# A sparse 3x3 convolution on one core: the seventh pair stored in halves, three input loads moved

## The chip, the core and the metric

The kernel runs on one core of a Trainium2 chip. The metric is the device time of one execution in microseconds (us); lower is better. The core has five engines with their own instruction streams: TensorE (PE in the profile, with its weight loads as PEld), VectorE (DVE), ScalarE (ACT), GpSimd (POOL) and SyncE (SP). DMA transfers are issued by SP and by POOL here and are moved by the core's 16 DMA engines.

## The reference

The input `x` is 16 images of 64 channels of 64 x 64 float32; `weight` is 128 x 64 x 3 x 3, nine tenths of it zero. With a padding of one pixel on each side:

```python
for b in range(batch):
    for co in range(c_out):
        for ci in range(c_in):
            for kh in range(k):
                for kw in range(k):
                    if weight[co, ci, kh, kw] != 0:
                        output[b, co] += weight[co, ci, kh, kw] * x_pad[b, ci, kh:kh+h, kw:kw+w]
```

The kernel computes it as a dense convolution. It reads 16.8 MB of float32 input and writes 33.6 MB of float32 output.

## The kernel before

**Tiling.** Two images make a pair: their 2 x 64 channels fill the 128 partitions. There are 8 pairs (numbered 0 to 7), and each pair is worked in 4 blocks of 16 output rows, so 32 blocks, `b` = 0 to 31. `xs` holds all 8 pairs in bf16 at once, so no load waits for a buffer. The output of a pair is built in one of three float32 tiles `os` (`p % 3`), 4 MB each.

**A block.** POOL adds neighbouring input rows into `s` (line 178), ACT copies the block's 18 rows into `win` (line 211), and PE makes three products from them (line 292): `ps_p`, shared by even and odd output rows, then `ps_e` and `ps_o`. ACT copies `ps_p` to `pc` (line 219); DVE adds it to `ps_e` and to `ps_o` and writes the even and odd rows of the output tile (line 248). A block takes PE 3.24 us.

**Stores.** After the last block of a pair DVE writes a small tile `mark` (line 254) whose only use is to raise the semaphore `r`. SP's stream is a list of stores, each waiting for its value of `r`: one store of 4 MB for each of pairs 0 to 6 (lines 116 to 119), and two of 2 MB, rows 0 to 31 and rows 32 to 63, for pair 7 (lines 121 to 128), the first of them after block 29. A whole store moves in runs of 16 KB, a half in runs of 8 KB. Before DVE writes the first block of pair 3 or later it waits until the store that last read the same output tile has landed (`st0` to `st2`, line 246).

**Loads.** SP loads the weights and the first 32 rows of pair 0 in float32. All other input comes through POOL's DMA queue, which converts float32 to bf16 on the way. POOL's stream holds these issues in a fixed order: the rest of pair 0, pairs 1 to 3 and 24 rows of pair 4 at the start, and the others behind the addition of a given block, by the table `AT` (lines 157 to 163): the rest of pair 4 behind block 6 (and after pair 0's output is complete), pair 5 behind block 10, pair 6 behind block 14, and the halves of pair 7 behind blocks 18 and 22. The semaphores of the loads are `x0` to `x4` (`p % 5`); POOL's addition and ACT's copy of a pair's first block wait for the value in `X_LANDS` (line 103). For pair 7 that is 48, so both its halves must have landed before block 28.

**End.** After the blocks, SP waits for all stores (lines 313 to 317).

Of the kernel before, what the change touches and what calls it, by code (L numbers as in the profile page):

```python
# [17 lines left out]
def kernel(  # L18
# [20 lines left out]
    TURN = 2  # L39
    HEAD = 32  # L40
    CUT = 24
    N_O = 3

    pool = ctx.enter_context(tc.tile_pool(name="all", bufs=1))
# [55 lines left out]
    def x_sem(p):  # L100
        return f"x{p % 5}"

    X_LANDS = {0: 16, 1: 16, 2: 16, 3: 16, 4: 32, 5: 32, 6: 32, 7: 48}
    HEAD_R, HEAD_C, HEAD_Q = 8, 4, 3
    R_OF = {p: HEAD_R + p + 1 for p in range(NP - 1)}

    with tc.tile_critical(no_gpsimd_drain=True):  # L107
        with nc.Block(no_gpsimd_drain=True) as block:  # L108

            @block.sync  # L110
            def _(sp):
                sp.dma_start(  # L112
                    out=w_sb, in_=weight.rearrange("o i kh kw -> o (i kh kw)")
                ).then_inc(S("w"), 16)
                sp.dma_start(out=x_head, in_=pair(0)[:, 0:HEAD, :]).then_inc(S("xh"), 16)
                for p in range(NP - 1):
                    after(
                        sp.dma_start(out=out_of(p), in_=os[p % N_O]), ("r", R_OF[p])
                    ).then_inc(S(f"st{p % N_O}"), 16)
                p = NP - 1  # L120
                for h in range(2):
                    rows = slice(32 * h, 32 * h + 32)
                    after(
                        sp.dma_start(
                            out=out_of(p)[:, :, rows, :], in_=os[p % N_O][:, :, rows, :]
                        ),
                        ("r", HEAD_R + NP + h),
                    ).then_inc(S("st7" if h else f"st{p % N_O}"), 16)

            @block.gpsimd  # L130
            def _(gp):
                def load(p, a, b, *waits):
                    after(
                        gp.dma_start(out=xs[:, p, a + 1 : b + 1, :], in_=pair(p)[:, a:b, :]), *waits  # L134
                    ).then_inc(S(x_sem(p)), 16)

                load(0, HEAD, H)
                gp.memset(ident, 0.0).then_inc(S("s"), 1)
                after(
                    gp.affine_select(  # L140
                        out=ident,
                        in_=ident,
                        compare_op=mybir.AluOpType.not_equal,
                        fill=1.0,
                        base=0,
                        pattern=[[-1, 128]],
                        channel_multiplier=1,
                    ),
                    ("s", 1),
                ).then_inc(S("s"), 1)  # L150
                for p in range(1, 4):
                    load(p, 0, H)
                load(4, 0, CUT)
                for _ in range(16):
                    gp.nop()

                AT = {
                    6: (4, CUT, H, ("r", R_OF[0])),
                    10: (5, 0, H),
                    14: (6, 0, H),  # L160
                    18: (7, 0, 32),
                    22: (7, 32, H),
                }
                for b in range(NB):
                    p, r0 = b // 4, 16 * (b % 4)
                    waits = []
                    if b == 0:
                        waits.append(("xh", 16))
                    if b == 2 or (b % 4 == 0 and b):
                        waits.append((x_sem(p), X_LANDS[p]))  # L170
                    if b >= 2:
                        waits.append(("p", b - 1))
                    if b < 2:
                        src = x_head[:, r0 : r0 + 16, :]
                    else:
                        src = xs[:, p, r0 + 1 : r0 + 17, :]
                    after(
                        gp.tensor_tensor(  # L178
                            out=ss[b % 2], in0=src[:, 0:16:2, :], in1=src[:, 1:16:2, :], op=ADD
                        ),  # L180
                        *waits,
                    ).then_inc(S("s"), 1)
                    if b in AT:
                        load(*AT[b])

            @block.scalar
            def _(act):
                after(cast_w(act.copy, G1, 3, 4), ("w", 16)).then_inc(S("c"), 1)
                cast_w(act.copy, G2, 0, 3).then_inc(S("c"), 1)
                after(act.copy(out=wT[:, G1], in_=wps(G1)), ("q", 1)).then_inc(S("c"), 1)  # L190
                after(act.copy(out=wT[:, G2], in_=wps(G2)), ("q", 3)).then_inc(S("c"), 1)

                def window(b):
                    p, r0 = b // 4, 16 * (b % 4)
                    parts = [(xs[:, p, r0 : r0 + 18, :], 0, [])]
                    if b == 0:
                        parts = [(x_head[:, 0:17, :], 1, [("xh", 16)])]
                    elif b == 1:
                        parts = [
                            (x_head[:, 15:32, :], 0, []),  # L200
                            (xs[:, 0, 33:34, :], 17, [(x_sem(0), X_LANDS[0])]),
                        ]
                    elif b == 2:
                        parts = [(x_head[:, 31:32, :], 0, []), (xs[:, 0, 33:50, :], 1, [])]
                    elif b % 4 == 0:
                        parts[0][2].append((x_sem(p), X_LANDS[p]))
                    if b >= 2:
                        parts[0][2].append(("q", HEAD_Q + 2 * (b - 2) + 2))
                    for k, (src, a, waits) in enumerate(parts):
                        copy = after(  # L210
                            act.copy(out=win[b % 2][:, a : a + src.shape[1], :], in_=src), *waits  # L211
                        )
                        if k == len(parts) - 1:
                            copy.then_inc(S("x"), 1)

                window(0)
                window(1)
                for b in range(NB):
                    after(act.copy(out=pcs[b % 2], in_=ps_p[b % 2]), ("p", b + 1)).then_inc(S("c"), 1)  # L219
                    if b + 2 < NB:  # L220
                        window(b + 2)

            @block.vector
            def _(dve):
                dve.memset(idle_rhs, 0.0).then_inc(S("r"), 1)  # L225
                dve.memset(xs[:, :, 0 : H + 2 : H + 1, :], 0.0)
                dve.memset(win[0][:, 0:1, :], 0.0).then_inc(S("r"), 1)
                after(cast_w(dve.tensor_copy, G1, 0, 3), ("w", 16)).then_inc(S("r"), 1)
                cast_w(dve.tensor_copy, G0, 0, 3)
                cast_w(dve.tensor_copy, G0, 3, 4).then_inc(S("r"), 1)  # L230
                cast_w(dve.tensor_copy, G2, 3, 4).then_inc(S("r"), 1)
                after(dve.tensor_copy(out=wT[:, G0], in_=wps(G0)), ("q", 2)).then_inc(S("r"), 1)  # L232
                after(
                    dve.tensor_tensor(out=wT[:, G01], in0=wps(G0), in1=wT[:, G1], op=SUB), ("c", 3)
                ).then_inc(S("r"), 1)
                after(
                    dve.tensor_tensor(out=wT[:, G21], in0=wps(G2), in1=wT[:, G1], op=SUB), ("c", 4)
                ).then_inc(S("r"), 1)
                for b in range(NB):
                    p, r0 = b // 4, 16 * (b % 4)  # L240
                    for k, src in enumerate((ps_e, ps_o)):
                        waits = [("q", HEAD_Q + 2 * b + k + 1)]
                        if k == 0:
                            waits.append(("c", HEAD_C + b + 1))
                            if b % 4 == 0 and p >= N_O:
                                waits.append((f"st{p % N_O}", 16 * (p // N_O)))
                        after(
                            dve.tensor_tensor(  # L248
                                out=os[p % N_O][:, :, r0 + k : r0 + 16 : 2, :], in0=src, in1=pcs[b % 2], op=ADD
                            ),  # L250
                            *waits,
                        ).then_inc(S("eo"[k]), 1)
                    if b % 4 == 3 or b == NB - 3:
                        dve.memset(mark, 0.0).then_inc(S("r"), 1)

            @block.tensor
# [54 lines left out]
                        pe.sem_inc(S(name), -TURN)  # L311

    sixteen = nc.sync.to_reg(16)
    done = {f"st{k}": 16 * len([p for p in range(NP) if p % N_O == k]) for k in range(N_O)}
    for name in sorted(done, key=lambda k: (done[k], k)):
        nc.sync.wait_ge(S(name), nc.sync.to_reg(done[name]), synchronizes=[nc.sync.lower_ap(o[:]) for o in os])
    nc.sync.wait_ge(S("st7"), sixteen, synchronizes=[nc.sync.lower_ap(o[:]) for o in os])
# [30 lines left out]
```

## Time and profile before

| | |
|---|---|
| median of 3 runs | 126.09 us (126.01 to 126.65) |
| the profiled execution's own time | 126.21 us |
| its span, first to last instruction | 124.4 us |
| PE busy | 109.6 us, 88% |
| DVE, ACT, POOL busy | 79.2, 69.3, 43.0 us |
| DMA engines: SP's queue, POOL's queue | 67.3% and 30.6% of 16 engines' span |
| last DVE addition ends | 113.9 us |
| last store issued, landed | 113.95 us, 123.5 us |

The span is 1.8 us shorter than the execution's time; this part lies around the first and last instruction. Times in the text are counted from the span's start. The profile's rate in GB/s counts a load by the bf16 bytes that it writes, half of the float32 bytes that it reads; the text says so where it adds both. The share of the DMA engines is the time that packets took; packets are put down to the window in which they start, so a short window can show a little more than 1.00.

### The profile page before, as it was taken

The page shows a single profiled execution, that of the slowest core. Times are in us where ns is not written, and L with a number is a line of the kernel's source. Part 1 is how long each engine was busy: PE and PEld are TensorE (multiplying, and loading weights), DVE is VectorE, ACT ScalarE, POOL GpSimd, SP SyncE. Part 2 cuts the span into 40 slices and gives each one's busy share as a digit, 9 for nine tenths or more (in the row PEclk, how much of TensorE's full clock was granted, in tenths as well). Part 3 has the DMA queues.
Part 4 walks back from the last instruction along what each step waited for, and adds up shares of the span by engine and source line. Part 5 has one row for each costly group of instructions (what it writes and reads, how often), then busy time and mean ns, then how long its engine had stood idle before and what let it go on. Part 6 is the DMA issues. An engine that isn't in the chain of part 4 may idle for free.

```text
span 124.4 us, 2437 instructions
## 1 busy us (share of the span) xinstructions
PE 109.6 (88%) x983; PEld 49.1 (39%) x983; DVE 79.2 (64%) x83; ACT 69.3 (56%) x71; POOL 43.0 (35%) x48
## 2 busy tenths in 40 slices
PE   5949999999999999999999999999999999992000
PEld 1414444444444444444444444444444444440000
DVE  2615676777677777777777767775867677775000
ACT  4564666666666666666666666657566666630000
POOL 5564333533353334433343334333333333000000
PEclk9999999999999999999999999999999999999855
DMA  3999999999999999999999999999999999999991
GB/s 85 375 225 213 211 219 219 239 438 338 332 363 432 308 329 324 387 353 345 298 379 408 321 369 427 413 367 348 433 421 432 427 384 427 458 390 416 413 419 71
DMA packets 4179, 42.79 MB, mean 344 GB/s; under 512 B 336, under 2 KB 336, under 8 KB 1104
## 3 DMA queue, kind: packets, MB, share of 16 engines
q1 hardware_dynamic: 2736, 34.90, 67.3%
q0 software_dynamic: 1440, 7.86, 30.6%
q14 instruction: 3, 0.02, 0.0%
HBM read 17.07 MB, written 33.55 MB: 407 GB/s over the span
## 4 chain that ended last, share of the span: by engine, by line
PE 84%; DMA 5%; POOL 1%; DVE 1%; SPq 0%; issue 0%; DVEq 0%
PE ps_e L292 33%; PE ps_o L292 33%; PE ps_p L292 17%; DMA x_head<-in_x_dram 5%; POOL s L178 1%; DVE o L248 1%; SPq L112 0%; SPq L343 0%; SPq L107 0%; DVEq L108 0%
## 5 line engine op out<-in xcount | busy, mean ns | idle before, releaser
L248 DVE TENSOR_TENSOR o<-ps_e,pc 128x1024 f32<-128x1024 f32 x32 | 39.2, 1225 | 31.2 <-ACT pc L219 22.9
L178 POOL TENSOR_TENSOR s<-xs 128x512 bf16<-128x512 bf16 x30 | 34.5, 1150 | 58.0 <-PE ps_p L292 58.0
L211 ACT COPY win<-xs 128x1152 bf16<-128x1152 bf16 (+2 forms) x31 | 34.7, 1121 | 34.2 <-PE ps_o L292 34.2
L292 PE MATMUL ps_e<-win,wT 64*128 64x504 bf16 (+1 forms) x384 | 46.8, 377 | 0.0
L292 PE MATMUL ps_o<-win,wT 64*128 64x504 bf16 (+1 forms) x384 | 46.8, 377 | 0.0
L248 DVE TENSOR_TENSOR o<-ps_o,pc 128x1024 f32<-128x1024 f32 x32 | 38.9, 1216 | 0.1
L219 ACT COPY pc<-ps_p 128x1024 f32<-128x1024 f32 x32 | 32.2, 1006 | 1.8 <-PE ps_p L292 1.8
L292 PEld LDWEIGHTS ps_o<-win,wT 64*128 64x128 bf16 x384 | 18.9, 94 | 22.6 <-DVE o L248 0.2
L292 PEld LDWEIGHTS ps_e<-win,wT 64*128 64x128 bf16 x384 | 18.8, 94 | 22.8 <-DVE o L248 0.8
L292 PE MATMUL ps_p<-s,wT 64*128 64x504 bf16 (+1 forms) x192 | 26.0, 377 | 1.6 <-POOL s L178 1.6
L292 PEld LDWEIGHTS ps_p<-s,wT 64*128 64x128 bf16 x192 | 9.4, 94 | 13.2 <-POOL s L178 2.1
L262 PE MATMUL ps_p<-idle_rhs 128*128 128x512 bf16 x14 | 4.8, 503 | 1.4 <-DVE idle_rhs L225 1.4
L134 POOL DMA_DIRECT2D xs<-in_x_dram x10 | 5.7, 573 | 1.0 <-SPq L107 1.0
L211 ACT CAST win<-x_head 128x1088 bf16<-128x1088 f32 (+1 forms) x3 | 2.3, 811 | 2.8 <-PE ps_o L292 1.6
L178 POOL TENSOR_TENSOR s<-x_head 128x512 bf16<-128x512 f32 x2 | 2.5, 1270 | 2.4 <-DMA x_head<-in_x_dram 2.4
L262 PEld LDWEIGHTS ps_p<-idle_rhs 128*128 128x128 bf16 x14 | 1.5, 117 | 3.4 <-DVE idle_rhs L225 1.4
L91 DVE CAST w_bf<-w_sb 128x192 bf16<-128x192 f32 (+1 forms) x4 | 1.1, 348 | 2.0 <-DMA w_sb<-in_weight_dram 2.0
L91 ACT ACT_TABLE_LOAD x1 | 1.3, 1283 | 0.9 <-SPq L107 0.9
L91 ACT CAST w_bf<-w_sb 128x64 bf16<-128x64 f32 (+1 forms) x2 | 0.7, 415 | 1.7 <-DMA w_sb<-in_weight_dram 1.7
L225 DVE MEMSET idle_rhs<- 128x256 uint32 x1 | 0.3, 272 | 1.1 <-SPq L107 1.1
L232 DVE CAST wT<-ps_e 128x384 bf16<-128x384 f32 x1 | 0.6, 557 | 0.3 <-PE ps_e L267 0.3
L190 ACT CAST wT<-ps_o 128x384 bf16<-128x384 f32 x1 | 0.5, 478 | 0.3 <-PE ps_o L267 0.3
(18 smaller groups left out, 5.4 us busy)
## 6 DMA issues: line engine op xcount, KB each, us to landing
out_dram<-o SPq DMA_DIRECT2D x7, 4096.0 KB, 17.3
xs<-in_x_dram POOLq DMA_DIRECT2D x5, 1024.0 KB, 16.3
out_dram<-o SPq DMA_DIRECT2D x2, 2048.0 KB, 10.3
xs<-in_x_dram POOLq DMA_DIRECT2D x3, 512.0 KB, 13.4
x_head<-in_x_dram SPq DMA_DIRECT2D x1, 1024.0 KB, 5.8
xs<-in_x_dram POOLq DMA_DIRECT2D x1, 640.0 KB, 14.2
xs<-in_x_dram POOLq DMA_DIRECT2D x1, 384.0 KB, 21.2
w_sb<-in_weight_dram SPq DMA_DIRECT2D x1, 288.0 KB, 2.9
```

Source lines behind the costliest of these rows:

```text
L91: return copy(out=w_bf4[:, g, a:b, :], in_=w_v[:, k : k + b - a, :])
L134: gp.dma_start(out=xs[:, p, a + 1 : b + 1, :], in_=pair(p)[:, a:b, :]), *waits
L178: gp.tensor_tensor(out=ss[b % 2], in0=src[:, 0:16:2, :], in1=src[:, 1:16:2, :], op=ADD),
L190: after(act.copy(out=wT[:, G1], in_=wps(G1)), ("q", 1)).then_inc(S("c"), 1)
L211: act.copy(out=win[b % 2][:, a : a + src.shape[1], :], in_=src), *waits
L219: after(act.copy(out=pcs[b % 2], in_=ps_p[b % 2]), ("p", b + 1)).then_inc(S("c"), 1)
L225: dve.memset(idle_rhs, 0.0).then_inc(S("r"), 1)
L232: after(dve.tensor_copy(out=wT[:, G0], in_=wps(G0)), ("q", 2)).then_inc(S("r"), 1)
L248: dve.tensor_tensor(out=os[p % N_O][:, :, r0 + k : r0 + 16 : 2, :], in0=src, in1=pcs[b % 2], op=ADD),
L262: mm = pe.matmul(idle_ps, idle_rhs[:, 0:128], idle_rhs, start=True, stop=True)
L292: mm = pe.matmul(dst[:, n, :, c_lo:c_hi], tap(g, kw, n), src[q, first : first + 7 * step + 1 : step, c_lo + kw - 1 : c_hi + kw - 1], start ...
```

## The change

Pair 6 is stored in two halves as pair 7 is: DVE also writes `mark` after block 25, and SP issues rows 0 to 31 then and rows 32 to 63 after block 27. SP's list of stores is now made from a list of parts, and the last waits count one store more for `st0`. Pair 5's load is issued behind block 7 instead of block 10, one block after the rest of pair 4. Pair 7's load is cut at row 36 instead of row 32, and its two pieces are issued behind blocks 22 and 25 instead of 18 and 22. Its second piece has a semaphore of its own, `xl`, and only block 30 waits for it (POOL's addition and ACT's copy); block 28 waits for the first piece alone.

```diff
+    LAST = 36
+    HALVES = (6, 7)
...
-    X_LANDS = {0: 16, 1: 16, 2: 16, 3: 16, 4: 32, 5: 32, 6: 32, 7: 48}
+    X_LANDS = {0: 16, 1: 16, 2: 16, 3: 16, 4: 32, 5: 32, 6: 32, 7: 32}
     HEAD_R, HEAD_C, HEAD_Q = 8, 4, 3
-    R_OF = {p: HEAD_R + p + 1 for p in range(NP - 1)}
+    parts = [(p, 32 * h, 32 * h + 32) for p in HALVES for h in range(2)]
+    parts = [(p, 0, H) for p in range(NP) if p not in HALVES] + parts
+    R_OF = {part[:2]: HEAD_R + k + 1 for k, part in enumerate(parts)}
...
-                for p in range(NP - 1):
+                for part in parts:
+                    p, a, b = part
                     after(
-                        sp.dma_start(out=out_of(p), in_=os[p % N_O]), ("r", R_OF[p])
-                    ).then_inc(S(f"st{p % N_O}"), 16)
...
+                        sp.dma_start(out=out_of(p)[:, :, a:b, :], in_=os[p % N_O][:, :, a:b, :]),
+                        ("r", R_OF[p, a]),
+                    ).then_inc(S("st7" if part == parts[-1] else f"st{p % N_O}"), 16)
...
-                    ).then_inc(S(x_sem(p)), 16)
+                    ).then_inc(S("xl" if (p, a) == (7, LAST) else x_sem(p)), 16)
...
                 AT = {
-                    6: (4, CUT, H, ("r", R_OF[0])),
-                    10: (5, 0, H),
+                    6: (4, CUT, H, ("r", R_OF[0, 0])),
+                    7: (5, 0, H),
                     14: (6, 0, H),
-                    18: (7, 0, 32),
-                    22: (7, 32, H),
+                    22: (7, 0, LAST),
+                    25: (7, LAST, H),
                 }
...
+                    if b == NB - 2:
+                        waits.append(("xl", 16))
...
+                    elif b == NB - 2:
+                        parts[0][2].append(("xl", 16))
...
-                    if b % 4 == 3 or b == NB - 3:
+                    if b % 4 == 3 or (p in HALVES and b % 4 == 1):
                         dve.memset(mark, 0.0).then_inc(S("r"), 1)
...
-    done = {f"st{k}": 16 * len([p for p in range(NP) if p % N_O == k]) for k in range(N_O)}
+    done = {f"st{k}": 16 * len([t for t in parts[:-1] if t[0] % N_O == k]) for k in range(N_O)}
```

More of the change, by code (lines that the diff above doesn't have):

```diff
@@ L115, in _ @@
                 sp.dma_start(out=x_head, in_=pair(0)[:, 0:HEAD, :]).then_inc(S("xh"), 16)
-                for p in range(NP - 1):
+                for part in parts:
+                    p, a, b = part
                     after(
-                        sp.dma_start(out=out_of(p), in_=os[p % N_O]), ("r", R_OF[p])
-                    ).then_inc(S(f"st{p % N_O}"), 16)
[L120 to L128, printed above, removed]
+                        sp.dma_start(out=out_of(p)[:, :, a:b, :], in_=os[p % N_O][:, :, a:b, :]),
+                        ("r", R_OF[p, a]),
+                    ).then_inc(S("st7" if part == parts[-1] else f"st{p % N_O}"), 16)
             @block.gpsimd
```

## The prediction

> **What bounds the kernel now.** I read the chain of waits first, then the busy slices of the DMA engines, then windows around the places where these show less than full, then the timeline of the engines that issue transfers.
>
> ```profile
> DMA  3999999999999999999999999999999999999991
> ...
> q1 hardware_dynamic: 2736, 34.90, 67.3%
> q0 software_dynamic: 1440, 7.86, 30.6%
> ...
> HBM read 17.07 MB, written 33.55 MB: 407 GB/s over the span
> ...
> PE 84%; DMA 5%; POOL 1%; DVE 1%; SPq 0%; issue 0%; DVEq 0%
> ```
>
> The chain names PE, with 84%. But the two queues together take 67.3 + 30.6 = 97.9% of 16 engines' span, and the DMA row is 9 in 38 of 40 slices. PE runs without a gap because its input always comes in time. What ends the run is what is left to move when PE is done: the last `mark` is written at 113.85 us, and the span lasts 10.5 us more.
>
> ```profile
> 113.85 0.06 DVE L254 MEMSET mark<- 128x1 f32 x1
> ```
>
> Windows of two stretches (start:end, length, the engines' busy times, granted clock, DMA share, GB/s) show where the DMA engines are not full:
>
> ```profile
> 96.00:99.00 3.00, 3.00 (x30) 1.37 (x28) 2.06 (x3) 2.06 (x2) 1.15 (x1) 1.00 1.01 431
> 99.00:102.00 3.00, 3.00 (x32) 1.37 (x28) 2.19 (x4) 2.06 (x2) 1.15 (x1) 1.00 0.88 377
> 102.00:105.00 3.00, 3.00 (x32) 1.36 (x28) 2.22 (x2) 2.05 (x2) 1.15 (x1) 1.00 1.01 426
> ...
> 118.00:121.00 3.00, 0.00 (x0) 0.00 (x0) 0.00 (x0) 0.00 (x0) 0.00 (x0) 0.50 1.01 421
> 121.00:122.00 1.00, 0.00 (x0) 0.00 (x0) 0.00 (x0) 0.00 (x0) 0.00 (x0) 0.50 0.81 336
> 122.00:123.00 1.00, 0.00 (x0) 0.00 (x0) 0.00 (x0) 0.00 (x0) 0.00 (x0) 0.50 0.08 33
> ```
>
> The reader is to see one dry spot, a share of 0.88 in 99 to 102 us, and a ragged end: the last 33 KB, four runs of 8 KB, move alone after 122 us. The dry spot has a cause in the timeline: pair 5's store has moved its data, and pair 6's is issued only after the last block of the pair, its `mark` being at 101.00 us. In half-microsecond windows the share is 0.76, 0.40, 1.08 and 1.23 from 101 on, so new data flow from about 102.0: 0.9 us after an issue at 101.10.
>
> So DMA work is conserved: 50.6 MB must pass, and moving a transfer gains only what it fills of a dry spot or of the ragged end. In 30 to 36 us, where a load and a store share the engines, the store queue moved 1.59 MB and the load queue 0.49 MB as bf16, 0.98 as float32: 2.57 MB in 6 us, 428 GB/s. Stores alone have 431, loads alone (12 to 22 us, 2.15 MB as bf16) 430. The mix has no price of its own.
>
> **Part 1, pair 6 in halves: the dry spot.** Block 25's second addition starts at 93.29 us and takes 1.22, so the first half is issued at about 94.6 and flows from 95.5 if the queue is free. Pair 5's store keeps the engines until about 101.7, so the spot is filled. On the mean of the engines it is worth (1 - 0.88) x 3 = 0.36 us. The end is set by the slowest engine, though, and an engine that lags has no gap there. From issue plus time to landing, the stores' last engines land at 93.4 (pair 4: 75.03 + 18.4), 103.4 (88.30 + 15.1) and 113.6 us (101.10 + 12.5): 10.0 us for a store without a dry spot before it, 10.2 for the one with it. Bounds: 0 (the slowest had no gap) and -0.36. I take -0.2, the difference of the landings, since landings are what ends the run.
>
> **Part 2, pair 6 in halves: smaller runs.** Pair 6 moves in runs of 8 KB instead of 16. Eight-KB runs pass at 420 GB/s (113 to 121 us, 3.36 MB), sixteen at 431: 4.194 MB takes 9.99 instead of 9.73 us, +0.25. By landings, pair 7's halves took 118.6 - 113.6 = 5.0 and 123.5 - 118.6 = 4.9 us, together 0.1 less than the whole store before the spot. Bounds -0.1 and +0.25; I take +0.2, nearer the packets, since the landings are rounded to 0.1.
>
> Its instructions lie beside other work. One more `mark` (59 ns) falls into DVE's 0.89 us of idle time before its addition at 95.39. One more issue on SP (0.37 us) stands 6.5 us ahead of the next. If DVE's cover were gone, 0.06 us would fall on a chain that has, at the end, 1.8 us to spare (below).
>
> **Part 3, pair 5's load behind block 7.** POOL issues it at about 26.9 us instead of 36.53; the 0.57 us lie in the 2.15 us that POOL waits for PE before its addition at 29.01. The rest of pair 4, issued at 23.57, lands 14.2 us later, at 37.8; pair 5's data then follow it in the same queue from about 36.5 instead of 41. The 2.1 MB move from one place in a full stream to another. Pair 0's store (23.16 + 15.4 = 38.6) shares the engines some 2 us longer and lands about 1 us later; DVE needs its tile only for pair 3, near 50 us. Pair 1's lands at 53.4 as before, as all that moves by then is the same. A load's start beside a store could cost: the first microsecond of the rest of pair 4's (28 to 29) has a share of 0.89, that of pair 5's (41 to 42) 0.98 and the next 0.86. But 39 to 45 us moved 1.81 MB of stores and 0.38 of bf16 loads, 2.57 as float32, 428 GB/s: against 431, 0.04 us lost. Bounds -0.05 (that start disappears) and +0.1 (as the 28 to 29 one); I take 0.
>
> **Part 4, pair 7's load later.** POOL's issues move to 75.43 (after block 22, unchanged in place) and 85.2 (block 25's addition starts at 84.06, and the issue follows 1.1 us later), 0.57 us within its wait of 2.09.
>
> ```profile
> 75.43 0.57 POOL L134 DMA_DIRECT2D xs<-in_x_dram  x1
> ...
> 84.06 1.15 POOL L178 TENSOR_TENSOR s<-xs 128x512 bf16<-128x512 bf16 x1 [2.02 <-PE ps_p L292]
> 87.30 1.15 POOL L178 TENSOR_TENSOR s<-xs 128x512 bf16<-128x512 bf16 x1 [2.09 <-PE ps_p L292]
> ```
>
> From an issue at 75.43 nothing had moved on POOL's queue by 79.5; say 4.7 us to first data. Then 0.41 MB of bf16 moved in 81 to 87 us, 68 GB/s. The first piece (36 rows, 0.59 MB) runs 80 to 88.8 and lands near 89.5; block 28 needs it at about 94. The second (28 rows, 0.46 MB) runs from 89.9 to 96.6 and lands near 97.6; behind `xl` stand POOL's addition of block 30 (100.40 now), its block 31, and ACT's copy (102.95). PE needs both at 106, so it would wait only for a landing after 104.8. Cost 0; the cover is 7 us.
>
> What is late or early next: without the early first half, pair 3's store lands 1.05 MB / 0.43 = 2.4 us sooner, near 79.4, and pair 4's, which no longer shares with the last 0.92 MB, 2.1 us sooner, near 91.3. Their successors can flow 0.9 us after their issues, at 75.9 and 89.2. Data end about 1 us before the last landing, so the margins are some 2.5 and 1.1 us (half of that for the engines in front), and no new dry spot opens. At the end 7b can flow from 113.95 + 0.9 = 114.9, while the engines reach it near 116.7: 1.8 us to spare.
>
> **Sum.** -0.2 + 0.2 + 0 + 0 = 0.0 us on the profiled execution's 126.21 (span 124.4 and 1.8 around it), which lies 0.12 above the median of 126.09. I predict 126.1.
>
> **The rivals.**
>
> *The ragged end closes (faster).* Full queues could let all engines finish together. For it: only four runs move after 122 us, so the end could come up to 1.0 us sooner, with 0.36 from the spot. Against: an engine that lags at 103.4 lags for the same reason still. It gives 126.1 - 1.0 + 0.2 = 125.3 at half the spot, 125.1 at best.
>
> *The slowest engine never ran dry.* Then the spot is worth 0 and the runs cost 0.25: 126.4. For it: three of the 16 closing packets of pair 5's store still fall into 102 to 103 us, so three engines passed to the next store without a gap. Against: its landings are 0.2 us further apart all the same.
>
> *Handing over between stores costs (slower).* The place is the borders 5/6a, 6a/6b and 6b/7a; the price is the 0.9 us from issue to first data for the one border that is new; it decides if an issued store cannot follow its predecessor's data directly. 126.1 + 0.9 = 127.0. Against: at the border 7a/7b (116 to 118 us) the stream does not thin; 115 to 118 moved 415 GB/s. The Trainium skill's page "DMA: Bandwidth & Descriptors" (section "Anatomy of one DMA — SWDGE (gpsimd) path") gives each DMA a fixed part of about 2 us beside its bytes; taken as exposed, one DMA more would make an estimate of 128.1 by that page, and the border 7a/7b speaks against its being exposed here.
>
> *The last piece of input comes late (slower).* Its place is block 30; each us of landing after 104.8 delays PE, and after 106.6, the spare time being used up, the end. The longest time to landing on the page, 21.2 us, behind 85.2 gives 106.4: nothing. It would take 23 us for 127.3.
>
> **How the numbers follow.** No change within 0.4 us: 0.58. The slowest engine's rival: 0.14. Faster by the closed end: 0.15. Handing over: 0.08. Late input: 0.05. About 0.5%, 0.63 us, is what a measurement here tells from no change. Faster is the third case; slower is the last two and a share of 0.02 of the second, where load starts cost 0.1 each as well; same is the rest, 0.70. The bounds of the parts sum to -0.36 - 0.1 - 0.05 = -0.5 and 0 + 0.25 + 0.1 = +0.35; the low end reaches halfway into the faster rival, 125.4, the high end to the first slower one, 126.9.
>
> **What would show it.** Right: the share in 99 to 102 us is 1.0; pair 7's first half of the store lands near 118.6 and the second near 123.5; POOL's block 30 has no wait for a load; PE stays without gaps. Wrong: a share well under 1 near 77, 89 or 107 us, a wait of POOL or ACT on `xs`, or a last landing before 122.9, which means that the ragged end closed.

## The result and the profile after

The changed kernel takes 126.80 us, the median of 22 runs (126.41 to 127.58); the kernel before, run beside it, 126.31 us (22 runs, 126.01 to 127.27). The ratio is 1.0036 with a 95% interval of 1.0018 to 1.0053: some 0.45 us slower, inside the half per cent that was called no change, and clear of zero. Here and below, executions more than 1.5% above the fastest of their kernel are left out of the ratios and the median spans. The profiled execution took 127.11 us with a span of 125.3.

The page of the changed kernel, DMA lines and chain:

```profile
DMA  3999999999999999999999999999999999999980
...
q1 hardware_dynamic: 3008, 34.90, 66.6%
q0 software_dynamic: 1440, 7.86, 30.9%
...
HBM read 17.07 MB, written 33.55 MB: 404 GB/s over the span
...
PE 83%; DMA 5%; POOL 1%; DVE 1%; SPq 0%; issue 0%; DVEq 0%
```

The same bytes and nearly the same shares: still a stream that never stops. The windows of the changed kernel, in the columns of before:

```profile
99.00:102.00 3.00, 3.00 (x32) 1.35 (x30) 2.19 (x4) 2.07 (x2) 1.15 (x1) 1.00 1.02 437
...
121.00:122.00 1.00, 0.00 (x0) 0.00 (x0) 0.00 (x0) 0.00 (x0) 0.00 (x0) 0.50 0.85 360
122.00:123.00 1.00, 0.00 (x0) 0.00 (x0) 0.00 (x0) 0.00 (x0) 0.00 (x0) 0.50 0.18 74
123.00:124.30 1.30, 0.00 (x0) 0.00 (x0) 0.00 (x0) 0.00 (x0) 0.00 (x0) 0.50 0.03 13
```

The dry spot is gone (1.02 against 0.88), as forecast. The ragged end is longer, not shorter: 74 KB after 122 us against 33, and some after 123. And the time was lost elsewhere. The transfers of both kernels in 39 to 42 us, packets, MB and share of each queue; first the kernel before:

```profile
q1 hardware_dynamic: 65, 1.06, 89.6%
q0 software_dynamic: 15, 0.12, 19.5%
```

then the changed kernel:

```profile
q0 software_dynamic: 47, 0.39, 80.0%
q1 hardware_dynamic: 33, 0.28, 22.8%
```

With loads counted as float32, before moved 1.06 + 0.24 = 1.30 MB in these 3 us, 433 GB/s. The changed kernel moved 0.28 + 0.78 = 1.06 MB, 353 GB/s, although the shares add to 102.8%: the engines are busy, but the packets take longer. 47 packets of the load queue took 80% of 48 engine-us, 817 ns each, against about 625 ns for the same size when nothing hinders them.

The packet records say what this is. Pair 0's store has moved its last data by 39.1 to 39.5 us on 14 of the 16 engines. Pair 1's store, issued at 36.19, moves its first at 40.9 to 41.5 us on most engines, at the earliest 4.7 us after its issue. In between pair 5's load has the engines alone, with packets of up to 1,289 ns. Before, the same store, issued at 36.13, followed pair 0's without a break near 37.8 us: at that border no load was in flight, since the rest of pair 4 had ended by 37 and pair 5's load began near 41.5. Looked at this way, the kernel before has no load in flight at any border between two whole stores; near 80.3 us a load begins just behind one, and near 67.5 us one begins while half of the engines still finish pair 2's store, but pair 3's had been issued 5.4 us earlier.

The loss stays to the end. Pair 5's store, issued at 88.36, lands 15.9 us later at 104.3 (before 103.4), and the last half, issued at 114.02, 10.4 us later at 124.4 (before 123.5): 0.9 us at both places.

### The profile page after: what moved, and what is told of

It is laid out like the page before. It is cut to its first block, busy times and chain, and to the rows that moved or that the text cites. A ratio compares the mean times of both kernels' runs of the same rounds, so it can differ in the third digit from the quotient of the medians.

```text
span 125.3 us, 2441 instructions
## 1 busy us (share of the span) xinstructions
PE 109.4 (87%) x983; PEld 48.8 (39%) x983; DVE 79.1 (63%) x84; ACT 69.3 (55%) x71; POOL 43.0 (34%) x48
## 4 chain that ended last, share of the span: by engine, by line
PE 83%; DMA 5%; POOL 1%; DVE 1%; SPq 0%; issue 0%; DVEq 0%
PE ps_e L293 33%; PE ps_o L293 33%; PE ps_p L293 17%; DMA x_head<-in_x_dram 5%; POOL s L177 1%; DVE o L249 1%; SPq L116 0%; SPq L344 0%; SPq L111 0%; DVEq L112 0%
```

## Experiments

Three readings were at hand: **A**, the early load of pair 5 costs; **B**, the smaller runs of pair 6's halves cost and filling the dry spot returns nothing; **C**, pair 7's later load costs. After the first four runs A became **H** (any border between stores with a load in flight costs) against **H2** (with a load in flight a store needs 3.4 to 4.8 us from issue to first data, and costs where its predecessor ends sooner).

Since a few tenths are near what the times can tell, each run is also read by its packet records: the time from one amount of moved data to another, loads as float32, as the mean of all engines. The stretches hold the first borders (9.4 to 21.2 MB, about 25 to 53 us), the middle (to 32 MB, 78 us), the border between pairs 4 and 5 (to 39.9 MB, 96.5 us), and the dry spot with the tail (to 50.2 MB, 121 us). The last column is from 50.2 MB to the last engine's last data.

| kernel | 9.4-21.2 MB | 21.2-32 | 32-39.9 | 39.9-50.2 | to the last engine | ratio to before, 95% | median span (before beside it) |
|---|---|---|---|---|---|---|---|
| before | 27.96 | 25.32 | 18.47 | 24.57 | 1.98 | | |
| changed | 28.62 | 25.20 | 18.50 | 24.10 | 2.73 | 1.0036 (1.0018-1.0053) | 125.0 |
| changed, again | 28.29 | 25.21 | 18.68 | 24.10 | 2.57 | 1.005 (1.0024-1.0076) | 125.15 (124.5) |
| load 5 early only | 28.19 | 25.27 | 18.49 | 24.44 | 2.38 | 1.0008 (0.9961-1.0055) | 124.6 (124.4) |
| halves only | 27.81 | 25.29 | 18.47 | 24.10 | 2.56 | 1.0021 (0.997-1.0072) | 124.65 (124.4) |
| load 7 late only | (28.91) | 25.24 | 18.98 | 24.32 | 1.90 | 1.0024 (0.997-1.0077) | 125.05 (124.4) |
| changed, load 5 back | (31.40) | (25.23) | (18.89) | (24.09) | (6.1) | 0.9979 (0.9926-1.0031) | 124.35 (124.4) |
| the same, again | 28.00 | 25.25 | 18.96 | 24.10 | 3.29 | 1.0046 (1.0017-1.0076) | 125.35 (124.5) |
| and load 7 nested | 28.07 | 25.23 | 18.66 | 24.14 | 2.31 | 0.9997 (0.9966-1.0029) | 124.5 (124.5) |

The bracketed numbers are not used. In the two executions with a bracketed first stretch the first 32 rows of input landed late (POOL waited 3.4 and 4.4 us for them, 2.4 before), so PE and the first store came late, and the engines ran dry near 25 us, after all early loads. The second of them took 130.25 us, and its 6.1 holds a packet recorded after the program's last instruction. The spans, first to last instruction, leave out the part around them, which varies from 1.7 to 3.0 us, so they tell the kernels apart better than the times do.

### One part at a time

Pair 5's load back:

```diff
-                    7: (5, 0, H),
+                    10: (5, 0, H),
```

> The changed kernel with pair 5's load put back behind block 10; all else as changed. Theory A (the loss is the slow stretch that pair 5's early load makes between 36 and 42 us, read from the traces as some 0.65 us): 0.45 to 0.7 us faster than the changed kernel, so level with the kernel before or up to 0.3 us faster, and no DMA rate under 350 GB/s (loads counted as float32) in 39 to 42 us. Theory B (the loss is the 8 KB runs of pair 6's halves, 0.25 us, with nothing got from the dry spot): as slow as the changed kernel, 1.002 to 1.005 of before. Theory C (the loss comes from pair 7's late load): the same as B.

The kernel before with pair 5's load early, and nothing else:

```diff
-                    10: (5, 0, H),
+                    7: (5, 0, H),
```

> The kernel before with pair 5's load behind block 7 and nothing else changed. Theory A: 0.5 to 0.8 us slower than before (1.004 to 1.006), with the slow stretch at 39 to 42 us; the dry spot near 101 us becomes smaller, as the engines come to it later. Theories B and C: within 0.1% of before.

The kernel before with pair 6 in halves (the changed kernel's list of parts with the loads, their waits and `X_LANDS` as before):

```diff
-                for p in range(NP - 1):
+                for part in parts:
...
-                    if b % 4 == 3 or b == NB - 3:
+                    if b % 4 == 3 or (p in HALVES and b % 4 == 1):
```

> The kernel before with pair 6 stored in halves and nothing else changed. Theory A with my two prices of the prediction (-0.2 for the dry spot, +0.2 for the runs): within 0.2 us of before. Theory B: 0.25 to 0.45 us slower (1.002 to 1.0035). The dry spot in 99 to 102 us is gone in either.

The kernel before with pair 7's load late (written as the changed kernel with the other parts undone):

```diff
-    HALVES = (6, 7)
+    HALVES = (7,)
...
-                    7: (5, 0, H),
+                    10: (5, 0, H),
```

> The kernel before with pair 7's load cut at row 36 and issued behind blocks 22 and 25, and nothing else changed. Theories A and B: within 0.1% of before, the dry spot near 101 us still there. Theory C: 0.3 us slower or more.

Measured: none of the four is told from before by its time; the intervals are half a per cent to each side. The packets tell more. With pair 5's load early alone, the window of 39 to 42 us shows the slow stretch again:

```profile
q0 software_dynamic: 48, 0.39, 72.2%
q1 hardware_dynamic: 28, 0.38, 30.1%
```

That is 0.38 + 0.78 = 1.16 MB, 387 GB/s, and the stretch to 21.2 MB is 0.23 us longer than before. A's place is right; its size, 0.5 to 0.8 us, was not met here (the median span is 0.2 us longer).

The halves alone fill the dry spot, and on the mean of the engines that is worth 24.57 - 24.10 = 0.47 us. But the last engine ends 2.56 instead of 1.98 us after the 50.2 MB: 0.58 is given back. By landings, pair 5's store is down at 103.2 and the last half at 123.3, 20.1 us later; before, 103.4 and 123.5, 20.1 us too. This trace is of the shortest of the four executions that count (spans of 124.3 to 125.5 us), so a loss of a few tenths in the others is not ruled out. B's price of the runs is smaller than thought: with pairs 6 and 7 both in 8 KB runs, 103 to 121 us moved 7.63 MB on the store queue (424 GB/s) here and 7.68 (427) in the changed kernel, against 7.53 (419) before, where half the runs are long.

The late load alone has a loss that neither A nor C had put there: 18.98 - 18.47 = 0.51 us at the border between the stores of pairs 4 and 5. In 91 to 94 us it moved 0.41 MB of stores and 0.37 of bf16 loads, 1.15 MB, 383 GB/s. Pair 5's store was issued at 89.3, and its first data came at 92.8 to 93.3, after the load had been alone for more than a microsecond. The second run of the kernel with pair 5's load back, below, shows the same at the same border. It may not be lost in every execution: three spans of this kernel are 124.2 to 124.7 us and three 125.4 to 125.7, and the trace is of one of the latter. This is the second place of one mechanism: what the border between pairs 0 and 1 is to pair 5's early load, the border between pairs 4 and 5 is to pair 7's late one.

### Is it the border, or the late issue?

The changed kernel with pair 1 in halves too, so that a store stands ready long before the border:

```diff
-    HALVES = (6, 7)
+    HALVES = (1, 6, 7)
...
-                                waits.append((f"st{p % N_O}", 16 * (p // N_O)))
+                                waits.append((f"st{p % N_O}", 16 * len([t for t in parts if t[0] < p and t[0] % N_O == p % N_O])))
```

(the parts sorted by pair)

> The changed kernel with pair 1 stored in halves too, so that its first half is issued near 29.7 us, 9 us before pair 0's store has moved its data, with pair 5's load in flight at that border as in the changed kernel. Theory H (any border between two stores that a load in flight overlaps costs time): loads still run alone near 39 to 41 us and the rate there (loads as float32) is under 400 GB/s; time as the changed kernel or 0.2 us more for the smaller runs. Theory H2 (with a load in flight a store needs 3.4 to 4.8 us from its issue to its first data, and it costs time only where its predecessor ends sooner than that): store data follow without a break, the rate stays above 415 GB/s in 38 to 42 us, and 0.3 to 0.6 us of the loss are gone.

The kernel before with pair 7's first half one block earlier:

```diff
-                    18: (7, 0, 32),
+                    17: (7, 0, 32),
```

> The kernel before with the first half of pair 7's load behind block 17 instead of 18, so that it is in flight (about 64 to 71 us) at the border between the stores of pairs 2 and 3 near 67.5 us. Pair 3's store is issued at 62.1, 5.4 us ahead of that border. Theory H: loads alone for a microsecond or more near 67 to 70 us and 0.3 us or more lost there. Theory H2: no break, at most 0.1 us lost.

The kernel before with pair 6's load one block earlier:

```diff
-                    14: (6, 0, H),
+                    13: (6, 0, H),
```

> The kernel before with pair 6's load behind block 13 instead of 14, so that it follows right behind pair 5's and is in flight (about 51 to 60 us) at the border between the stores of pairs 1 and 2 near 53 us. Pair 2's store is issued at 49.1, 3.9 us ahead. Theory H: 0.3 us or more lost in 51 to 56 us, as with pair 5's early load. Theory H2: its first data at 52.5 to 53.9 us, so between nothing and 0.3 us lost.

Measured: H falls; H2 fits these three better, with limits. With pair 1 in halves, 39 to 42 us read:

```profile
q0 software_dynamic: 63, 0.47, 75.2%
q1 hardware_dynamic: 57, 0.35, 29.3%
```

0.35 + 0.94 = 1.29 MB, 430 GB/s, with pair 5's load in flight at the border all the same. Over 38 to 42 us, the stretch that was named ahead, it is 412 GB/s, just under the 415 expected. Pair 1's first half, issued at 30.4, follows at 39.5 us right after pair 0's last data, and the load's packets keep their 624 ns at first. In the 9.5 us that begin 12.5 us after the first store's issue it moved 0.55 us' worth less than 430 GB/s would. The two traces of the changed kernel have 0.92 and, below, 0.54, the kernel before 0.22, so this sum does not show a gain. Most of the 0.55 is at 38.0 to 38.7, where the load starts and the store's packets take 859 ns. The time shows no gain either: 127.11 us in 10 runs, 1.0046 (1.0009 to 1.0083), with a median span of 125.05 us against 124.3 for the kernel before beside it, and with pair 1 in 8 KB runs as well. Its profiled execution also ran dry near 25 us (its stretch to 21.2 MB takes 29.25 us), and what kept the others slow was not found. So this run shows that a store issued early can follow directly beside a load, and no more.

The other two have a load in flight at a later border, where the next store was issued 4.5 us ahead (pair 6's load) and 6.9 us (pair 7's). The first of them, 52.5 to 55.5 us:

```profile
q0 software_dynamic: 48, 0.39, 62.4%
q1 hardware_dynamic: 46, 0.49, 39.7%
```

0.49 + 0.78 = 1.27 MB, 423 GB/s; the other moved 0.75 + 0.52 = 1.27 MB in 67 to 70 us. Their stretches to 32 MB take 25.27 and 25.29 us (before 25.32), and single runs 126.22 and 126.10 us. In these two executions a border with a load in flight costs nothing when the store was issued early enough.

### A load in flight at the first store

Pair 6 in halves, and pair 4 loaded whole at the start:

```diff
-    CUT = 24
+    CUT = 64
...
-                    6: (4, CUT, H, ("r", R_OF[0, 0])),
```

> The kernel before with pair 6 stored in halves and pair 4 loaded whole at the start (no separate rest of pair 4 behind block 6). A load's start beside a running store shows slow packets in every trace (28 to 30 us here), about 0.2 us; one such start is taken away. If each load start costs so much: 0.2 us faster than the kernel with the halves alone, so level with or 0.2 us under before. If pair 0's store now suffers from the load in flight at its own start: 0.3 us or more lost near 25 to 29 us, and no gain.

Of the two outcomes expected it is the slower, and clearly: 127.43 us in 10 runs, 1.008 (1.0041 to 1.0118), with a median span of 125.55 us against 124.3. In 24 to 28 us:

```profile
q0 software_dynamic: 75, 0.61, 96.3%
q1 hardware_dynamic: 7, 0.11, 6.8%
```

Pair 0's store, issued at 23.11, moved its first data near 27.2, 4.1 us later (before: 1.5 us, with only the end of a load in flight), and the load, alone, fell to 0.11 + 1.22 = 1.33 MB in 4 us, 333 GB/s; 75 packets took 96.3% of 64 engine-us, 822 ns each. The stretch to 21.2 MB is 28.54 us, 0.73 more than with the halves alone. No predecessor's end is involved here, so it is the start of a store beside a load in flight.

### Putting the loads back between the borders

The last four ran side by side: the changed kernel itself; pair 5's load back behind block 10; that with pair 7's second piece behind block 26 instead of 25; and the changed kernel with pair 5's load behind block 9.

> The changed kernel itself, beside the next three. Theory H2 (with a load in flight a store needs 3.4 to 4.8 us from its issue to its first data; where its predecessor ends sooner, loads run alone and slowly): the slow stretch at 39 to 42 us is there again, 0.3 to 0.9 us lost against 430 GB/s between 36 and 45 us, and the time is 1.002 to 1.005 of before.

> The changed kernel with pair 5's load back behind block 10. H2: 0.2 to 0.6 us faster than the changed kernel beside it; nothing lost at the first border between stores, but up to 0.5 us at the border between the stores of pairs 4 and 5 near 90 to 93 us, where pair 7's late second piece is in flight and pair 5's store is issued only some 2 us ahead. If the loss of the changed kernel is not pair 5's load: level with it.

```diff
-                    7: (5, 0, H),
+                    10: (5, 0, H),
...
-                    25: (7, LAST, H),
+                    26: (7, LAST, H),
```

> As the kernel before it here, with pair 7's second piece behind block 26 instead of 25, so that its data start after pair 5's store has. H2: nothing lost at the border near 91 us, 0 to 0.4 us faster than the kernel before it; PE does not wait, as the piece lands by about 101 us and is needed at 104.8. If a late load costs by itself: no better.

```diff
-                    7: (5, 0, H),
+                    9: (5, 0, H),
```

> The changed kernel with pair 5's load behind block 9 instead of 7: its data come near 38 us, when pair 1's store is already prepared with no load in flight. H2: nothing lost in 36 to 45 us beyond the 0.2 us of any load's start, and 0.3 to 0.6 us faster than the changed kernel. If pair 5's load costs because it is early: a loss between those of block 7 and block 10.

Measured: the changed kernel is 1.005 of before, with the slow stretch again (39 to 42 us: 0.46 + 0.78 = 1.24 MB, 413 GB/s, spread wider). Pair 5's load back does not help the median by itself: 1.0046. The gain expected of it, 0.2 to 0.6 us, was missed, and the reason is in the table: it is quick to 21.2 MB (28.00) and then pays 18.96 instead of 18.47 us at the border of pairs 4 and 5. In 90 to 93 us that kernel reads:

```profile
q0 software_dynamic: 114, 0.37, 73.7%
q1 hardware_dynamic: 36, 0.46, 37.2%
```

0.46 + 0.74 = 1.20 MB, 400 GB/s. In the changed kernel the same window moved 0.59 + 0.72 = 1.31 MB, 437. There the delay suffered at 40 us makes pair 4's store end later (91 us instead of 90), while pair 5's is issued at the same time, near 88.4; so it has more lead, and its first data near 92 come almost in time. One loss pays for the other. A second difference is in the packets: in the changed kernel those of the load keep 285 to 289 ns at this border, though the load has most engines alone for over half a microsecond; with pair 5's load back some take up to 1,816 ns. This kernel's spans, too, lie apart: five are 124.3 to 124.7 us and seven 125.2 to 126.0, and the trace, at 125.7, is of one of the seven.

With both loads out of the way of both borders the time is 126.32 us, 0.9997 (0.9966 to 1.0029) of before: the loss is gone. Ten of its eleven spans lie between 124.3 and 124.6 us; those of the changed kernel beside it reach from 124.4 to 126.0. Its 90 to 93 us read:

```profile
q1 hardware_dynamic: 76, 1.16, 95.9%
q0 software_dynamic: 11, 0.04, 6.5%
```

Pair 5's store follows here without a break, and pair 7's second piece begins behind it, at 92.2. This kernel keeps the halves, the cut at row 36 and the late load of pair 7; it is level with the kernel before, and none of the kernels that ran is faster than that one beyond its interval.

Block 9 for pair 5's load was a miss, for H2 too. Its data come at 37.9 us, as planned, right behind pair 0's last data (37.9 to 38.6 on 15 engines). Yet pair 1's store, issued at 36.17 with only the end of pair 4's load in flight, moves its first data at 39.9 us, 3.7 us after its issue; in the kernel before, issued at 36.13, it took under 2. In 39 to 42 us this kernel reads:

```profile
q0 software_dynamic: 46, 0.38, 69.1%
q1 hardware_dynamic: 27, 0.43, 33.8%
```

That is 0.43 + 0.76 = 1.19 MB, 397 GB/s, and 28.35 us to 21.2 MB. At this border the difference to the kernel before is that pair 5's load had been issued ahead of the store, at 33.3 us, where before it was issued 0.4 us after it. With pair 5's load back behind block 10 it is the same at the border of pairs 4 and 5: the load was issued at 85.2 and the store at 88.3, and the load's data began at 89.6. So "a load in flight" is too narrow: by these two traces it is enough that a load has been issued before the store and has most of its data still to move. No run was made to test this further.

Its time, 127.60 us and 1.0091 (1.0059 to 1.0124), is mostly in the span: the nine spans are 124.8 to 126.6 us, median 125.4, against 124.5 for the kernel before. The profiled execution, with 124.9, is one of the shortest and has 2.7 us around its span where others have 1.8. What makes the rest of the nine so long stays open.

## Why the prediction was right, and where it was not

The forecast was no change: 126.1 us and a range of 125.4 to 126.9. The median is 126.80, near the upper end, and the change 0.36%, inside the 0.5%. The direction inside that band was not forecast. The bounds of the parts ended at +0.35 us, and the medians differ by 0.49: that the range holds the result is owed to its upper end, which was set by a rival that looked at other borders. The number is right in part by luck.

- **What bounds the kernel** held: PE kept its pace, no load was waited for (POOL's block 30 started at 100.53, with a wait for PE only), and all that moved the end was the DMA stream.
- **Part 1, the dry spot**, was filled. Its worth was taken as -0.2 us. It is -0.47 on the mean of the engines and nothing at the end, because the engines that lag were never dry. The rival of the slowest engine named this, at a chance of 0.14, and it is what the one trace of the halves alone shows.
- **Part 2, the smaller runs**, was mis-sized: +0.2 was taken from 420 GB/s in the tail of before, which was also slow for its long runs. At the 427 GB/s of the changed kernel, 4.194 MB cost 9.82 instead of 9.73 us, +0.09.
- **Part 3, pair 5's load**, is the step that failed: "The 2.1 MB move from one place in a full stream to another", with a bound of +0.1 us. It cost 0.23, 0.33 and 0.66 us in three profiles. I counted bytes and asked which tile would be late, but not what is in flight when the next store starts. "Pair 1's lands at 53.4 as before" went wrong with it: pair 0's store landed at 41.0 and pair 1's at 55.2 us.
- **Part 4, pair 7's load**: 0 was taken, and PE indeed never waited. It costs 0.5 us at the border of pairs 4 and 5 when pair 5's load is in its old place (in the executions that were traced), and 0.03 to 0.2 in the changed kernel, where the earlier loss hides it.
- **"Their successors can flow 0.9 us after their issues"** is the same error as a number. The 0.9 us came from the one start in the trace that has no load beside it (issued 101.10, flowing from 102.0). With a load issued ahead that has most of its data still to move it is 3.4 us (pair 5's store) to 4.7 us (pair 1's). "The mix has no price of its own" was read from 30 to 36 us, where nothing starts. Pair 3's store landed at 79.4 as forecast, pair 4's at 93.0 instead of 91.3.
- **Handing over costs** had the right kind of cause at the wrong borders. It looked at the borders of the last stores, where no load is in flight; those stay free of cost. The fixed 2 us for each DMA, which the Trainium skill's page "DMA: Bandwidth & Descriptors" (section "Anatomy of one DMA — SWDGE (gpsimd) path") gives, does not show there: 103 to 121 us hold three borders at 427 GB/s. That section is about DMAs of the GpSimd path, and these stores are issued by SP.
- **The ragged end** did not close; it grew.
- **The signs to look for**: the landings told it. Pair 7's halves were to land near 118.6 and 123.5 us and landed at 119.5 and 124.4. The share of the DMA engines, the other sign I had named, is 1.03 in 39 to 42 us of the changed kernel, since packets that take longer count as busy; the place of the loss shows only in the bytes.

The sum of 0.0 us was thus near the truth for the halves (0 at the end of the one trace, with other terms) and short by the cost of the loads, 0.2 to 0.7 us at the first border.

## What to carry to other kernels

In a kernel bound by its transfers, bytes are conserved but the rate is not: look at each border between two transfers of one queue and at what the other queue has in flight there. Count in what has only been issued. Either let the other queue's transfer lie between the borders, or issue the next transfer well ahead of its predecessor's end (4.5 and 6.9 us were enough in the two executions that tried it). Filling a dry spot shifts the mean of the engines; the end moves only if the engine that ends last was dry too, and undoing one of two losses may only uncover the other.

## What was not expected of the hardware

- A store's time from issue to first data was 0.9 us with no load beside it, 1.5 us beside the end of a load, and 3.4 to 4.7 us where a load had been issued ahead of it and had most of its data still to move (the first store of the kernel with pair 4 whole, pair 1's and pair 5's in the others).
- While such a store is being prepared, the load's packets can slow down though they have the engines alone: 817 and 822 ns on average at two such places, up to 1,324, against 625. Not at every one: at the border of pairs 4 and 5 the changed kernel's load packets kept 285 to 289 ns. The same is seen the other way about: in the microsecond before the first data of the loads near 28 and 41 us, the kernel before's store packets of 16 KB take 739 and 790 ns on average and up to 1,207, instead of 611; before the loads near 54, 67 and 80 us they take 612 to 628. Why a start slows what is already moving, and only at some places, is open.
- Engines that get equal work end 1.2 to 2.8 us apart, by the mark that each engine records at the end of a store. In the second run with pair 5's load back this spread was 1.1 us at the end of pair 3's store, 3.3 at that of pair 4's, where pair 7's second piece starts, and 2.8 at the end; from pair 5's store on, the first and the last engine both took 4.9 us for each half, so the lag was only carried along. In the kernel with the halves alone the spread grew from 1.0 us at the end of pair 4's store to 2.1 at the end of the run. What gives one engine the lag was not settled.
